# Griffin and attention trunk on one core: another loading order at the start, matmuls of ones ahead, and the first row sum two units later

## The chip, the cores and the metric

The kernel runs on one core of one Trainium2 chip. The metric is the device time of one execution in microseconds. All inputs and weights are fp32 and lie in HBM; about 404 MB are read in each execution.

## What is computed

A trunk of two layers works on T = 288 tokens (32 of a running stream, 256 of a new prompt) with a width of 2048. Layer 0 mixes with a gated linear recurrence, layer 1 with differential attention; a gated MLP with a short convolution follows each. Only layer 0's mixer is touched by the change:

```python
def rms_norm(x, g):
    return x * rsqrt(mean(x * x, -1) + EPS) * g

def rglru_mixer(x, conv_hist, h0, w_in, conv_w, conv_b, gate_w, gate_b, log_lam, w_out):
    u = x @ w_in                                   # x after rms_norm; 2048 -> 4096
    y = gelu(u[..., :2048])                        # "g" tiles
    full = concat([conv_hist, u[..., 2048:]])      # "r" tiles
    xc = causal_dwconv(full, conv_w, conv_b)       # width 4
    g = sigmoid(einsum('btnc,ncd->btnd', blocks(xc), gate_w) + gate_b)
    r, i = halves of g
    log_a = -8 * r * softplus(-log_lam)
    a = exp(log_a); b = sqrt(-expm1(2 * log_a)) * i * xc
    h_t = a_t * h_(t-1) + b_t                      # linear recurrence over the tokens
    return (h * y) @ w_out
```

## The kernel before

The width of 2048 is kept as 16 chunks of 128 partitions, so x is 16 tiles of 128x288; a DMA brings two chunks, 288 KB, and x0 to x7 below are these pairs. To reach fp32 accuracy, every operand is cut into a high and a low part, and each chunk of a product takes three matmuls into one PSUM bank: high by high (L967), weight-high by x-low (L968), weight-low by x-high (L969).

The weights stream once. They come in **units** of 2, 4 or 8 chunks of one output tile. For each unit SP issues the load (L840, tiles `w` for the small units 0 to 7, a ring of four `wr` buffers from unit 8 on), ACT rounds the high part (`cut_hi`, L845, `wh`), DVE subtracts it for the low part (`cut_lo`, L850, `wl`), and PE runs the unit's matmuls: 24 for a unit of 8 chunks. The chunks of x are cut in the same way at the start: `xh` on ACT (L144, scaled by the norm constants in `crg`) and `xl` on DVE (L147). The norm's own factor is applied later, when a tile leaves PSUM.

The main loop runs over the units in order. At unit i it issues the load of unit i+5, ACT's cut of unit i+3, then all side work that is due at i (`S.run_due(i)`, from a table filled with `S.at` and `S.chain`), then DVE's cut of unit i+3, then the matmuls of unit i. Each engine works off its own list in that order, so side work that stands ahead of a cut delays it, and with it the unit three further on.

The first four output tiles (r0, r1, g0, g1) are interleaved: units 0 to 3 are their first 2 chunks, 4 to 7 the next 2, 8 to 11 the next 4 and 12 to 15 the last 8. Their four PSUM banks come free only after the norm's factor is known: squares of x (`first_sq`, L157 on ACT, added up on DVE at L161), a matmul with ones over all partitions (`norm_row`, L205 and L206), and an inverse root on DVE (L181 to L198). `norm_row` is due at unit 14. From unit 16 on a tile is two units of 8 chunks (r2, r3, r4, r5, g2, g3, r6, r7, and so on).

Behind each r tile n stands a chain of stages: s1 evacuates PSUM (L330, L331) and loads the gate weights, s2 is the convolution (three DVE operations at L340 behind one on ACT), s3 and s4 cut its result and the gate weights (`xch`, `gwh` on ACT, `gwl`, `xcl` on DVE), s6 runs six gate matmuls (L362 to L364), s7 is four ACT operations with the sigmoid table, s8 a reciprocal on DVE (L379), s9 one ACT operation, s10 (odd n) a square root with its own table (L393), s11 the scans on DVE (L400, L402). Behind a g tile stands the gelu (L422), with a third table. `ACT_TABLE_LOAD` is the change from one of these tables to another.

Before the loop, ACT's queue issues the loads of x0, of the first norm constants `crg`, of x1, and later x2 and x3; SP's queue issues units 0 to 7, the rest of `crg`, units 8 to 11 and then x4 to x7. `coef` (due at unit 5) works out constants of the recurrence on ACT, POOL and DVE. In `psS` lie two PSUM banks for scores, which in layer 0 serve the gates of even tiles as `gate_ps`.

Of the kernel before, what the change touches and what calls it, by code (L numbers as in the profile page):

```python
# [11 lines left out]
F32 = mybir.dt.float32  # L12
# [6 lines left out]
P = 128  # L19
D = 2048  # L20
NS, NP = 32, 256
T = NS + NP
KC = D // P
# [6 lines left out]
LAM0 = 0.8 - 0.6 * math.exp(-0.3 * 1)  # L30
SCALE = 128.0 ** -0.5

REC_W = 296
REC_N = 292
REC_P = 36
# [61 lines left out]
def trunk(ctx, tc, d, prefetch=5, ahead=3):  # L97
    nc = tc.nc
    S = Stream()
# [7 lines left out]
    psA = ctx.enter_context(tc.tile_pool(name="psA", bufs=2, space=bass.MemoryType.PSUM))  # L107

    xx = [main.tile([P, 2 * T], F32, tag=f"x{c}", name=f"x{c}") for c in range(KC // 2)]
    x = [xx[c // 2][:, (c % 2) * T:(c % 2 + 1) * T] for c in range(KC)]  # L110
    xh = [main.tile([P, T], F32R, tag=f"xh{c}", name=f"xh{c}") for c in range(KC)]
# [42 lines left out]
    def first_sq(c):  # L154

        t = rgp.tile([P, 2 * T], F32, tag="ssw", name="ssw", bufs=1) if c == 0 else (nvz, srb)[c % 2]
        nc.scalar.activation(t, xx[c], AF.Square)  # L157
        if c == 0:
            acc_box["w"], acc_box["a"], acc_box["b"] = t, t[:, 0:T], t[:, T:2 * T]
        else:  # L160
            nc.vector.tensor_add(acc_box["w"], acc_box["w"], t)  # L161
# [41 lines left out]
    def norm_row(key):  # L203
        ps = psA.tile([P, 512], F32, tag="A", name="ssq_ps")
        nc.tensor.matmul(ps[:, :T], ones, acc_box["a"], start=True, stop=False)  # L205
        nc.tensor.matmul(ps[:, :T], ones, acc_box["b"], start=False, stop=True)  # L206
        rb_box["r"], *steps = rsqrt_steps(ps[:, :T], D, "rb")
        for f in steps:
            f()
        S.done.add((key, "r"))  # L210
# [108 lines left out]
    def rec_done(n):  # L319
        def done(i, ps):  # L320
# [62 lines left out]
                e["a"] = rgp.tile([P, REC_N], F32, tag="a", name="a", bufs=4)  # L383
                nc.scalar.activation(e["a"], e["q"], AF.Copy, scale=2.0, bias=-1.0)

            w = (1, 2, 1, 1)[n] if n < 4 else 0
            stages = [(1, s1), (2, s2), (3, s3), (4, s4)]
            stages += [(t + w, f) for t, f in ((6, s6), (7, s7), (8, s8), (9, s9))]
            if k == 1:
                def s10():  # L390
# [15 lines left out]
                        S.done.add(("hs", q))  # L406
                    return f
                stages += [(10 + w, s10), (11 + w, s11(n - 1)), (12 + w, s11(n))]
            S.chain(i + (1 if n < 2 else 0), *stages)
        return done  # L410

    def gate_done(n):
        def done(i, ps):
            e = {}
            k = n % 2

            def s1():
                e["y"] = rgp.tile([P, T], F32, tag="y", name="y", bufs=4)
                evac_scaled(e["y"], ps[:, :T], "n0")

            def s2():
                nc.scalar.activation(e["y"], e["y"], AF.Gelu_apprx_tanh)  # L422

            def s3():
                nc.gpsimd.tensor_mul(e["y"], e["y"], rgs[n]["hs"])

            def s4():
                nc.scalar.activation(Hh[n], e["y"], AF.Copy)

            def s5():  # L430
                nc.vector.tensor_sub(Hl[n], e["y"], r32(Hh[n]))  # L431
                S.done.add(("H0", n))
            w = 0 if k else 2
            S.at(i + 1, s1)
            S.at(i + 2 + w, s2)
            due = [i + 3 + w]

            def poll():
                if ("hs", n) in S.done:
                    s3()  # L440
                    S.chain(due[0], (1, s4), (2, s5))
                else:
                    due[0] += 1
                    S.at(due[0], poll)
            S.at(due[0], poll)
        return done
# [291 lines left out]
    def need_of(key):  # L738
        return lambda k: (key, k)

    order = [("r", 0), ("r", 1), ("g", 0), ("g", 1), ("r", 2), ("r", 3)]
    for n in range(4, KC, 2):
        order += [("r", n), ("r", n + 1), ("g", n - 2), ("g", n - 1)]
    order += [("g", KC - 2), ("g", KC - 1)]
    tiles = [tile_units(d["w_in"], n + (KC if w == "r" else 0), 0, [8, 8] if n >= 2 else [2, 2, 4, 8],
                        xh, xl, need_of("n0"), rec_done(n) if w == "r" else gate_done(n))
             for w, n in order]
    phase(tiles, 4)

    def open_pool(name, old):  # L750
# [101 lines left out]
    def cutw(u):  # L852
        cut_hi(u)
        cut_lo(u)

    nc.vector.memset(ones, 1.0)
    for b in recbuf:
        nc.gpsimd.memset(b, 0.0)

    def load_x(eng, *pairs):  # L860
        for c in pairs:
            eng.dma_start(xx[c], d["x"][c])

    def split_x(a, b):
        for c in range(a, b):
            norm_hi(c, rg("norm", c))
            norm_lo(c, rg("norm", c), "n0")

    def square_x(a, b):
        for c in range(a // 2, b // 2):  # L870
            first_sq(c)

    def coef():

# [14 lines left out]
        nc.gpsimd.tensor_scalar(o, l, -4.0, 0.0, op0=OP.mult, op1=OP.max)  # L889
        nc.gpsimd.tensor_add(o, o, q)  # L890

    load_x(nc.scalar, 0)
    nc.scalar.dma_start(crg[:, 0:KC], d["p_rg"][:, 0:KC])
    load_x(nc.scalar, 1)
    for i in range(12):
        tag = "hs" if i < 4 else "y"
        load(units[i], rgp.tile([P, T], F32, tag=tag, name="w0", bufs=4) if i < 8 else None)
        if i == 7:
            nc.sync.dma_start(crg[:, KC:], d["p_rg"][:, KC:])
    load_x(nc.sync, 4, 5, 6, 7)  # L900
    make_identity(nc, ident)
    cutw(units[0])
    split_x(0, 2)
    load_x(nc.scalar, 2)
    cutw(units[1])
    load_x(nc.scalar, 3)
    for u in units[2:4]:
        cutw(u)

    def side_loads():  # L910
# [9 lines left out]
        nc.vector.tensor_scalar(lam[:, 3:4], lam[:, 2:3], -LAM0, None, op0=OP.add)  # L920
        nc.vector.tensor_scalar(subc, rg("sub", 0, 2), 1.0 - LAM0, None, op0=OP.mult)

    for t, c, n in ((1, 2, 2), (3, 4, 2), (5, 6, 2), (7, 8, 4), (8, 12, 4)):
        S.at(t, lambda c=c, n=n: split_x(c, c + n))
    for t, c, n in ((9, 0, 4), (10, 4, 4), (11, 8, 4), (12, 12, 4)):
        S.at(t, lambda c=c, n=n: square_x(c, c + n))
    S.at(5, coef)
    S.at(14, lambda: norm_row("n0"))
    S.at(24, side_loads)
    S.at(40, lam_setup)  # L930

# [147 lines left out]
```

## Time and profile before

| | us |
|---|---|
| median of three runs (2507.55 to 2507.96) | 2507.75 |
| the profiled execution | 2507.55 |
| its span (first to last instruction) | 2505.7 |
| PE busy | 2480.6 (99%) |
| DVE busy | 1626.6 (65%) |
| ACT busy | 1198.3 (48%) |
| share of PE in the chain that ended last | 96% |

The profiled execution is 1.85 us longer than its span; that part lies outside all instructions. "Busy" counts an engine's instructions on their own, so PE at 99% says that hardly any time is left between matmuls, wherever they wait. Which stretch holds what is left is told by the list of PE's waits and by the timeline, where the bracket behind an instruction is the idle time ahead of it and what released it.

### The profile page before, as it was taken

What the parts mean: (1) busy time and instruction counts of PE and PEld (TensorE: products, weight loads), DVE (VectorE), ACT (ScalarE), POOL (GpSimd) and SP (SyncE); (2) the same over time, 40 slices, a digit from 0 to 9 for tenths busy, and PEclk for the clock granted to TensorE, in tenths of its full rate; (3) what the DMA queues carried; (4) which work ended last, traced back from release to release, by engine and by line L of the source; (5) the groups of instructions that cost most, each with busy time, mean ns of one, the idle gap of its engine ahead of it and who ended that gap; (6) DMA issues with size and microseconds to landing.
All of it is one profiled execution on the core that took longest, in us unless ns stands there. A gap on an engine that the chain in (4) does not pass through costs nothing.

```text
span 2505.7 us, 45997 instructions
## 1 busy us (share of the span) xinstructions
PE 2480.6 (99%) x18567; PEld 2474.0 (99%) x18567; DVE 1626.6 (65%) x2596; ACT 1198.3 (48%) x1749; POOL 279.0 (11%) x770
## 2 busy tenths in 40 slices
PE   8999999999999999999999999999999999999997
PEld 8999999999999999999999999999999999999997
DVE  8987666666446666555677677766666446666543
ACT  6887444444334444444445444544444334444442
POOL 3544110000000000011000000210000000000021
PEclk9999999999999999999999999999999999999999
DMA  6444444444554444555544553544445554444553
GB/s 227 165 163 163 168 163 164 165 166 159 166 166 169 165 164 168 158 164 174 181 161 161 176 171 115 194 161 168 163 165 161 164 170 165 166 165 164 162 168 115
DMA packets 126358, 414.36 MB, mean 165 GB/s; under 512 B 14400, under 2 KB 22976, under 8 KB 126144
## 3 DMA queue, kind: packets, MB, share of 16 engines
q1 hardware_dynamic: 124416, 409.39, 49.6%
q8 instruction: 145, 2.38, 0.4%
q10 hardware_dynamic: 1728, 2.02, 0.2%
q14 instruction: 69, 0.57, 0.1%
HBM read 403.86 MB, written 7.50 MB: 164 GB/s over the span
## 4 chain that ended last, share of the span: by engine, by line
PE 96%; DVE 1%; ACT 1%; issue 0%; DMA 0%; POOL 0%; ACTq 0%; DVEq 0%; POOLq 0%
PE acc L967 31%; PE acc L969 31%; PE acc L968 31%; DVE wl L850 0%; ACT wh L845 0%; PE os_ps L689 0%; PE spare L967 0%; DMA crg<-p_rg 0%; PE spare L969 0%; PE spare L968 0%; PE osq_ps L718 0%; PE sc_ps L557 0%; PE sc_ps L555 0%; PE sc_ps L556 0%; PE gate_ps L363 0%
## 5 line engine op out<-in xcount | busy, mean ns | idle before, releaser
L845 ACT ACTIVATE wh<-wr 128x1024 fp32r<-128x1024 f32 (+2 forms) x776 | 799.3, 1030 | 1206.4 <-PE acc L968 850.9
L850 DVE TENSOR_TENSOR wl<-wr,wh 128x1024 fp32r<-128x1024 f32 (+2 forms) x776 | 925.3, 1193 | 510.1 <-ACT wh L845 509.5
L967 PE MATMUL acc<-xh,wh 128*128 128x288 f32 x4096 | 1217.3, 297 | 6.2 <-ACT xh L144 6.2
L968 PE MATMUL acc<-xl,wh 128*128 128x288 f32 x4096 | 1209.6, 295 | 0.0
L969 PE MATMUL acc<-xh,wl 128*128 128x288 f32 x4096 | 1206.0, 294 | 2.5 <-DVE wl L850 2.5
L969 PEld LDWEIGHTS acc<-xh,wl 128*128 128x128 f32 x4096 | 772.3, 189 | 3.5 <-DVE wl L850 3.4
L967 PEld LDWEIGHTS acc<-xh,wh 128*128 128x128 f32 x4096 | 768.8, 188 | 6.8 <-ACT xh L144 6.2
L968 PEld LDWEIGHTS acc<-xl,wh 128*128 128x128 f32 x4096 | 770.0, 188 | 0.8 <-DVE xl L147 0.3
L968 PE MATMUL acc<-Hl,wh 128*128 128x288 f32 x1504 | 443.9, 295 | 0.8 <-DVE Hl L431 0.8
L967 PE MATMUL acc<-Hh,wh 128*128 128x288 f32 x1504 | 444.4, 295 | 0.0
L969 PE MATMUL acc<-Hh,wl 128*128 128x288 f32 x1504 | 442.9, 294 | 0.0
L968 PEld LDWEIGHTS acc<-Hl,wh 128*128 128x128 f32 x1504 | 282.3, 188 | 1.3 <-DVE Hl L431 1.2
L969 PEld LDWEIGHTS acc<-Hh,wl 128*128 128x128 f32 x1504 | 283.0, 188 | 0.0
L967 PEld LDWEIGHTS acc<-Hh,wh 128*128 128x128 f32 x1504 | 281.8, 187 | 0.1
L473 DVE SCALAR_TENSOR_TENSOR c<-up,cff,c 128x290 f32<-128x290 f32 x352 | 182.7, 519 | 6.2
L467 POOL COPY st_ff<-up 128x2 f32<-128x2 f32 x176 | 34.7, 197 | 1339.1 <-DVE up L463 1339.1
L462 DVE TENSOR_TENSOR up<-acc,srb 128x32 f32<-128x32 f32 x176 | 33.7, 192 | 128.7 <-PE acc L969 128.7
L967 PE MATMUL acc<-Hhx,wh 128*128 128x288 f32 x384 | 113.7, 296 | 0.0
L968 PE MATMUL acc<-Hlx,wh 128*128 128x288 f32 x384 | 113.3, 295 | 0.0
L969 PE MATMUL acc<-Hhx,wl 128*128 128x288 f32 x384 | 112.9, 294 | 0.0
L465 ACT ACTIVATE c<-up,cff 128x290 f32<-128x290 f32 x176 | 108.6, 617 | 0.7 <-DVE up L463 0.7
L172 POOL TENSOR_TENSOR srb<-srb,sq 128x288 f32<-128x288 f32 x56 | 62.0, 1107 | 287.0 <-ACT sq L165 281.4
(227 smaller groups left out, 1651.5 us busy)
## 6 DMA issues: line engine op xcount, KB each, us to landing
wr<-w_up SPq DMA_DIRECT2D x352, 512.0 KB, 3.7
wr<-w_dn SPq DMA_DIRECT2D x128, 448.0 KB, 3.3
wr<-w_qkv SPq DMA_DIRECT2D x96, 512.0 KB, 4.3
wr<-w_dn SPq DMA_DIRECT2D x64, 512.0 KB, 3.5
wr<-w_in SPq DMA_DIRECT2D x60, 512.0 KB, 3.8
wr<-w_rg_out SPq DMA_DIRECT2D x32, 512.0 KB, 3.7
wr<-w_at_out SPq DMA_DIRECT2D x24, 512.0 KB, 4.3
wr<-w_at_out SPq DMA_DIRECT2D x16, 256.0 KB, 3.2
```

The lines of the kernel that those rows point to most:

```text
L172: nc.gpsimd.tensor_add(acc_box["a"], acc_box["a"], sq)
L462: nc.vector.tensor_mul(buf[:, 2:34], ps[:, 0:NS], rb[:, 0:NS])
L465: nc.scalar.activation(c, buf[:, 0:UP_N], AF.Identity, scale=ff(f"w{l}", f), bias=ff(f"b{l}", f))
L467: nc.gpsimd.tensor_copy(st_ff[:, f, 0, :], buf[:, 290:292])
L473: nc.vector.scalar_tensor_tensor(c, buf[:, t:t + UP_N], ff(f"w{l}", t * 2 * NF + f), c, op0=OP.mult, op1=OP.add)
L845: nc.scalar.activation(u["wh"][:, :n], u["raw"][:, :n], AF.Copy)
L850: nc.vector.tensor_sub(u["wl"][:, :n], u["raw"][:, :n], r32(u["wh"])[:, :n])
L967: nc.tensor.matmul(o, wh, h, start=u["first"] and z == 0, stop=False)
L968: nc.tensor.matmul(o, wh, lo, start=False, stop=False)
L969: nc.tensor.matmul(o, wl, h, start=False, stop=u["last"] and z == nk - 1)
```

## The change

- ACT's queue issues the norm constants first, then the two halves of x0. All the other x pairs move to SP's queue, between the weights: x1 after unit 3, x2 and x3 after unit 7 (then the rest of `crg`), x4 after unit 9, x5 after unit 10, x6 and x7 after unit 11.
- Seven fp32 matmuls of ones with ones, 128 columns each, are PE's first work. Their bank is not read.
- The cuts of x8 to x15 (chunks) go to units 7, 8, 9 and 10, two each; they stood at 7 and 8, four each. The squares are due one by one at units 11, 11, 12, 12, 13, 14, 14 and 15; they stood in pairs at 9 to 12.
- `norm_row` is due at unit 16 (`ROW0`), not 14. The fifth and sixth output tiles (r2 and r3, units 16 to 19) accumulate in the two `psS` banks.
- The stages of r0 to r5 get new due times, and `gate_done` counts from unit 15 at the earliest. The gate matmuls of r0 to r7, which were due at units 20, 22, 24, 26, 27, 29, 35 and 37, are due at 22, 24, 26, 28, 30, 32, 35 and 37; the reciprocals follow two units behind.

The core of the diff:

```diff
+ROW0 = 16
...
-            w = (1, 2, 1, 1)[n] if n < 4 else 0
-            stages = [(1, s1), (2, s2), (3, s3), (4, s4)]
+            w = (1, 2, 3, 3, 1, 1)[n] if n < 6 else 0
+            v = w if n > 1 else 0
+            stages = [(1, s1), (2, s2), (3 + v, s3), (4 + v, s4)]
...
-            S.chain(i + (1 if n < 2 else 0), *stages)
+            S.chain((ROW0 - 1, ROW0, i, i, i + 2, i + 2)[n] if n < 6 else i, *stages)
...
             w = 0 if k else 2
+            i = max(i, ROW0 - 1)
             S.at(i + 1, s1)
...
-                        xh, xl, need_of("n0"), rec_done(n) if w == "r" else gate_done(n))
-             for w, n in order]
+                        xh, xl, need_of("n0"), rec_done(n) if w == "r" else gate_done(n),
+                        t - 4 if t in (4, 5) else None)
+             for t, (w, n) in enumerate(order)]
...
+    warm = psA.tile([P, 512], F32, tag="A", name="warm")
+    for _ in range(7):
+        nc.tensor.matmul(warm[:, 0:P], ones, ones, start=True, stop=True)
...
-    load_x(nc.scalar, 0)
     nc.scalar.dma_start(crg[:, 0:KC], d["p_rg"][:, 0:KC])
-    load_x(nc.scalar, 1)
+    for c in range(2):
+        nc.scalar.dma_start(x[c], d["x"][0][:, c * T:(c + 1) * T])
...
-        if i == 7:
+        if i == 3:
+            load_x(nc.sync, 1)
+        elif i == 7:
+            load_x(nc.sync, 2, 3)
             nc.sync.dma_start(crg[:, KC:], d["p_rg"][:, KC:])
-    load_x(nc.sync, 4, 5, 6, 7)
+        elif i in (9, 10):
+            load_x(nc.sync, i - 5)
+    load_x(nc.sync, 6, 7)
...
-    for t, c, n in ((1, 2, 2), (3, 4, 2), (5, 6, 2), (7, 8, 4), (8, 12, 4)):
+    for t, c, n in ((1, 2, 2), (3, 4, 2), (5, 6, 2), (7, 8, 2), (8, 10, 2), (9, 12, 2), (10, 14, 2)):
         S.at(t, lambda c=c, n=n: split_x(c, c + n))
-    for t, c, n in ((9, 0, 4), (10, 4, 4), (11, 8, 4), (12, 12, 4)):
-        S.at(t, lambda c=c, n=n: square_x(c, c + n))
+    for c in range(KC // 2):
+        S.at((11, 11, 12, 12, 13, 14, 14, 15)[c], lambda c=c: first_sq(c))
     S.at(5, coef)
-    S.at(14, lambda: norm_row("n0"))
+    S.at(ROW0, lambda: norm_row("n0"))
```

**SP's queue at the program's start.** `w` and `wr` are weights of units, `x_` a pair of x (the number names an instance, x_78 being x0), `crg` constants. Before:

```order
L840 DMA w_174<-w_in 128x256
L840 DMA w_176<-w_in 128x256
L840 DMA w_178<-w_in 128x256
L840 DMA w_180<-w_in 128x256
L840 DMA w_182<-w_in 128x256
L840 DMA w_184<-w_in 128x256
L840 DMA w_186<-w_in 128x256
L840 DMA w_188<-w_in 128x256
L899 DMA crg<-p_rg 128x226
L840 DMA wr<-w_in 128x512 x4
L862 DMA x_82<-x 128x576
L862 DMA x_83<-x 128x576
```

After:

```order
L845 DMA w_182<-w_in 128x256
L845 DMA w_184<-w_in 128x256
L845 DMA w_186<-w_in 128x256
L845 DMA w_188<-w_in 128x256
L871 DMA x_79<-x 128x576
L845 DMA w_191<-w_in 128x256
L845 DMA w_193<-w_in 128x256
L845 DMA w_195<-w_in 128x256
L845 DMA w_197<-w_in 128x256
L871 DMA x_80<-x 128x576
L871 DMA x_81<-x 128x576
L907 DMA crg<-p_rg 128x226
```

The x loads now stand among the weights that are used at the same time, x2 and x3 ahead of unit 8's weights.

**DVE around the row sum.** `ssw` adds up the squares, L181 to L198 (L182 to L199 after) are the inverse root, `rec` is the first evacuation. Before:

```order
L161 TENSOR_TENSOR ssw<-ssw,srb 128x576
L850 TENSOR_TENSOR wl<-wr,wh 128x1024 x2
L181 TENSOR_SCALAR nvz<-ssq_ps 128x288
L184 TENSOR_SCALAR srb<-nvz 128x288
L189 TENSOR_TENSOR nvz<-srb 128x288
L190 TENSOR_TENSOR nvz<-nvz 128x288
L191 SCALAR_TENSOR_TENSOR nvz<-nvz 128x288
L192 SCALAR_TENSOR_TENSOR srb<-nvz,srb 128x288
L196 TENSOR_TENSOR nvz<-srb 128x288
L197 SCALAR_TENSOR_TENSOR nvz<-nvz 128x288
L198 SCALAR_TENSOR_TENSOR srb<-nvz,srb 128x288
L330 TENSOR_TENSOR rec_165<-acc,srb 128x32
```

After:

```order
L162 TENSOR_TENSOR ssw<-ssw,srb 128x576
L855 TENSOR_TENSOR wl<-wr,wh 128x1024
L182 TENSOR_SCALAR nvz<-ssq_ps 128x288
L185 TENSOR_SCALAR srb<-nvz 128x288
L190 TENSOR_TENSOR nvz<-srb 128x288
L191 TENSOR_TENSOR nvz<-nvz 128x288
L192 SCALAR_TENSOR_TENSOR nvz<-nvz 128x288
L193 SCALAR_TENSOR_TENSOR srb<-nvz,srb 128x288
L197 TENSOR_TENSOR nvz<-srb 128x288
L198 SCALAR_TENSOR_TENSOR nvz<-nvz 128x288
L199 SCALAR_TENSOR_TENSOR srb<-nvz,srb 128x288
L331 TENSOR_TENSOR rec_165<-acc,srb 128x32
```

The last addition stood two weight cuts ahead of the inverse root; now it stands one cut ahead, and all of it two units later in the program.

**ACT about units 28 and 29.** `t` is the square root, `y` the gelu, `xch` and `gwh` are s3 and `r`, `ip`, `t`, `q`, `a` the set with the sigmoid table. Before:

```order
L393 ACT_TABLE_LOAD
L393 ACTIVATE t<-t 128x292 x2
L345 ACTIVATE xch<-xc 128x292
L140 ACTIVATE gwh<-gwr 128x256
L845 ACTIVATE wh<-wr 128x1024
L370 ACT_TABLE_LOAD
L370 ACTIVATE r<-gate_ps,crg 128x292
L371 ACTIVATE ip<-gate_ps,crg 128x292
L373 ACTIVATE t<-r,spc 128x292
L375 ACTIVATE q<-t 128x292
L384 ACTIVATE a<-q 128x292
```

After:

```order
L396 ACT_TABLE_LOAD
L396 ACTIVATE t<-t 128x292 x2
L850 ACTIVATE wh<-wr 128x1024
L425 ACT_TABLE_LOAD
L425 ACTIVATE y<-y 128x288
L346 ACTIVATE xch<-xc 128x292
L141 ACTIVATE gwh<-gwr 128x256
L425 ACTIVATE y<-y 128x288
L371 ACT_TABLE_LOAD
L371 ACTIVATE r<-gate_ps,crg 128x292
L372 ACTIVATE ip<-gate_ps,crg 128x292
L374 ACTIVATE t<-r,spc 128x292
```

A gelu with its table load now stands between the square root and the cuts `xch` and `gwh`, and a second one behind them.

## Rows read from the trace of the kernel before

**Rows 1.** Timeline of PE, start: begin, duration, instruction, [idle before <-releaser].

```profile
6.24 0.61 PE L967 MATMUL acc<-xh,wh 128*128 128x288 f32 x1 [6.24 <-ACT xh L144]
...
12.23 0.30 PE L969 MATMUL acc<-xh,wl 128*128 128x288 f32 x1
12.36 0.29 PE L967 MATMUL acc<-xh,wh 128*128 128x288 f32 x1
...
16.35 0.40 PE L969 MATMUL acc<-xh,wl 128*128 128x288 f32 x1 [0.38 <-DVE wl L850]
```

**Rows 2.** Timeline of PE, units 12 and 14.

```profile
24.50 0.40 PE L969 MATMUL acc<-xh,wl 128*128 128x288 f32 x1 [1.03 <-DVE wl L850]
...
31.42 0.75 PE L205 MATMUL ssq_ps<-ssw,ones 128*128 128x288 f32 x2 [0.52 <-DVE ssw L161]
32.01 0.65 PE L206 MATMUL ssq_ps<-ssw,ones 128*128 128x288 f32 x2
32.28 0.51 PE L967 MATMUL acc<-xh,wh 128*128 128x288 f32 x1
```

**Rows 3.** Timeline of PE, units 34 and 37.

```profile
102.57 0.40 PE L969 MATMUL acc<-xh,wl 128*128 128x288 f32 x1 [0.85 <-DVE wl L850]
...
114.39 0.40 PE L363 MATMUL gate_ps<-xcl,gwh 128*128 128x292 f32 x1 [1.14 <-DVE xcl L350]
```

**Rows 4.** Timeline of ACT, start.

```profile
5.65 0.96 ACT L144 ACTIVATE xh<-x,crg 128x288 fp32r<-128x288 f32 x2 [0.52 <-DMA crg<-p_rg]
...
13.27 0.63 ACT L845 ACTIVATE wh<-wr 128x512 fp32r<-128x512 f32 x1 [0.42 <-DVE wl L850]
```

**Rows 5.** Two windows: each engine's busy us (instructions), PEclk, DMA share, GB/s.

```profile
0.00:12.00 12.00, 5.76 (x23) 5.50 (x23) 4.43 (x12) 6.34 (x14) 1.27 (x8) 1.00 0.77 239
12.00:16.00 4.00, 3.97 (x29) 3.73 (x28) 2.99 (x8) 3.43 (x9) 0.44 (x2) 1.00 1.00 362
```

**Rows 6.** Timeline of DVE around units 8 and 12.

```profile
15.66 1.25 DVE L850 TENSOR_TENSOR wl<-wr,wh 128x512 fp32r<-128x512 f32 x2
...
22.53 0.76 DVE L161 TENSOR_TENSOR ssw<-ssw,srb 128x576 f32<-128x576 f32 x1 [0.97 <-ACT srb L157]
23.21 1.24 DVE L850 TENSOR_TENSOR wl<-wr,wh 128x1024 fp32r<-128x1024 f32 x1
```

**Rows 7.** DMA issues, 16.3 to 16.5 us: count, size, median us to landing.

```profile
wr<-w_in SPq DMA_DIRECT2D x1, 512.0 KB, 3.8
```

**Rows 8.** Timeline of DVE, first evacuation of a recurrent tile.

```profile
37.94 0.41 DVE L331 TENSOR_TENSOR rec<-acc,srb 128x256 f32<-128x256 f32 x1
```

**Rows 9.** Timeline of DVE, units 26 to 35.

```profile
64.76 1.64 DVE L340 SCALAR_TENSOR_TENSOR xc<-rec,crg,xc 128x292 f32<-128x292 f32 x3 [0.37 <-ACT xc L333]
...
67.45 1.97 DVE L379 RECIPROCAL q<-q 128x292 f32<-128x292 f32 x1
...
78.92 0.94 DVE L141 TENSOR_TENSOR gwl<-gwr,gwh 128x256 fp32r<-128x256 f32 x1 [2.00 <-ACT gwh L140]
79.78 0.45 DVE L239 TENSOR_TENSOR y<-acc,srb 128x288 f32<-128x288 f32 x1
80.15 1.21 DVE L850 TENSOR_TENSOR wl<-wr,wh 128x1024 fp32r<-128x1024 f32 x1
...
82.06 0.43 DVE L350 TENSOR_TENSOR xcl<-xc,xch 128x292 fp32r<-128x292 f32 x1
...
97.07 0.82 DVE L400 TENSOR_TENSOR_SCAN hs<-a,crg,ip 128x32 f32<-128x32 f32 x1 [0.78 <-POOL ip L394]
...
98.64 2.74 DVE L340 SCALAR_TENSOR_TENSOR xc<-rec,crg,xc 128x292 f32<-128x292 f32 x3 [0.15 <-ACT xc L333]
```

**Rows 10.** Timeline of ACT, units 28 to 31.

```profile
76.16 1.28 ACT L393 ACT_TABLE_LOAD   x1
...
88.53 0.78 ACT L422 ACTIVATE y<-y 128x288 f32<-128x288 f32 x2
...
89.89 1.04 ACT L845 ACTIVATE wh<-wr 128x1024 fp32r<-128x1024 f32 x1
```

More of the change, by code (lines that the diff above doesn't have):

```diff
@@ L867, in split_x @@
             norm_lo(c, rg("norm", c), "n0")
-    def square_x(a, b):
-        for c in range(a // 2, b // 2):
-            first_sq(c)
     def coef():
@@ L903, in trunk @@
     split_x(0, 2)
[L904 to L907, printed above, removed]
+    for u in units[1:4]:
         cutw(u)
```

## The prediction

> **What bounds the kernel now.** Read first the page's busy shares and the chain that ended last: PE is busy 99% of the span and the chain runs over PE for 96%. So only two things can move the time: idle time between matmuls, and matmuls that run slowly. The list of PE's waits sorts the idle time by what it waited for, the timeline says where each wait stands. What the change touches lies in the first 115 us, in two places.
>
> *The front*, up to unit 16. PE's first matmul starts at 6.24, behind the high cut of x. The 24th starts at 12.23 and the next at 12.36 [rows 1]: 23 spacings take 5.99 us, 0.26 each, against 0.13 between those two. This is the lower of the clock's two levels (1.2 GHz against 2.4) after an idle start; at 0.133 they would take 3.06, so it costs 2.93 us. PE then waits 0.38 for unit 8 at 16.35, 1.03 for unit 12 at 24.50, and 0.52 for the last addition of squares at 31.42 [rows 1, 2].
>
> *The middle*, units 26 to 37. PE waits 0.85 for unit 34 at 102.57 and 1.14 for a gate at 114.39 [rows 3]. After that no wait belongs to the parts that change.
>
> In both places PE is fed by a queue that cannot be made shorter by making PE faster: what is gained ahead of a wait is given back at the wait. So the forecast follows the last wait of each place, not the sum of all of them.
>
> **Part by part.**
>
> *Constants first, x0 in halves.* ACT's first cut of x begins at 5.65 after 0.52 us of waiting for `crg`, which was issued second [rows 4]. Issued first it lands earlier by one issue, at most those 0.52, while the half of x0 is issued where `crg` stood. PE's first matmul moves to about 5.75 to 5.9. By the rule above this is given back unless unit 8 comes earlier too.
>
> *Seven matmuls of ones.* No such matmul stands in the trace. Bounds: the pair of fp32 matmuls of 288 columns at L205 takes 0.59 from start to start of the next pair (31.42 to 32.01), so 0.3 each [rows 2]; at the lower clock twice that, 0.6. Seven at no more than 0.6 are 4.2 us, and since they need only a tile of ones they end before 5.75: they lie wholly in time in which PE stands still, cost 0. What they can bring is the clock: between 0 and 2.93 us on PE itself. The granted clock column is no help, it reads 1.00 for the first 12 us, where the spacing says half [rows 5]; hence I read the level from the spacing alone. That the engine was idle ahead of its slow stretch and had worked through it when it sped up is what [rows 1] show.
>
> The Trainium skill, "TensorE: Matmul & The Clock Gate", section "What's actually happening", says that the default state is throttled and activity releases it; by that rule PE reaches its first real matmul at full speed. The trace agrees on the order of things (slow first, fast after work). By that rule alone, without the next limit, the sum would be 2.9 us better.
>
> *The next limit: unit 8.* Its weights are cut on ACT at 13.27, its matmul starts at 16.35 [rows 1, 4]: 3.1 us, in which ACT cuts x6 and x7 and the constants of `coef`, and DVE gets to `wl` at 15.66 only behind a reciprocal that waits for POOL [rows 6]. None of this is moved: the order of ACT and DVE in this stretch is the same. What can come earlier is the cut at 13.27, and that follows the landing. 2.6 MB must land before it (units 0 to 8, x0 to x3, the constants); before, 239 GB/s over the first 12 us make 2.87 MB, and from 12 to 16 the DMA engines are 1.00 busy at 362 GB/s [rows 5]. The same bytes come in an order that only puts x ahead: 2.6 MB have landed at 10.9 by the mean rate, and I allow a spread to 12.2. The matmul of unit 8 can then stand at 14.9 to 15.4 with a fast clock. If the clock stays low until 12, the buffers of the small units hold ACT back (the cut at 13.27 itself waited 0.42 for DVE), and it comes at 15.6 to 15.7. So the warm-up, worth 2.93 on PE, is worth some 0.5 at unit 8.
>
> *Unit 12, the last wait of the front.* Its load needs the buffer that unit 8's low cut frees, at 16.3, and took 3.8 us to land [rows 7], at 20.2; the matmul that waits for its low cut starts at 24.50 [rows 2], 4.3 later. The change frees the buffer 0.65 (low clock) to 1.4 us (high) earlier. Behind the landing, one addition of squares no longer stands ahead of this cut on DVE; it held the queue from 22.53 to 23.21 [rows 6], and its square on ACT goes too: 0.6. Together 1.25 to 2.0. Against it, DMA is saturated until about 18 us by the same bytes, with x6 and x7 ahead of this load now as before; that takes up to 0.3. I take 1.4, range 0 (the landing does not move) to 2.0. Everything won earlier is inside this number.
>
> *Row sum at unit 16.* PE had nothing to do from 30.90 (31.42 less 0.52), and the next unit's matmul starts at 32.28, 1.38 later; since matmuls overlap by 0.16 (0.29 long, 0.13 apart), the loss is 1.54 [rows 1, 2]. The four row sum matmuls themselves take 0.86 of it (31.42 to 32.28) and are still to be done, the remaining 0.68 is the wait. Two units later the last addition is due at unit 15, one cut ahead of the row sum, and done some 2.4 us into that unit's 3.2 of matmuls: gain 0.68, bounds 0 and 0.68.
>
> *Two tiles in the score banks.* The inverse root begins behind the row sum, and the first tile was evacuated by 38.35, 6 us after the row sum [rows 2, 8]. With the row sum at unit 16 the four old banks come free about two units into the next tile; r2 and r3 have banks of their own until unit 20, 12.8 us after. Cost 0; without that cover PE would stand still for about 5 us. The banks are wanted again by the first gate at unit 22, when the evacuation of r3 at 20 is done with a margin of about 1.5 us: 0 again, with the price of a rival below.
>
> *New due times in the middle.* The work of DVE and ACT is the same, its order is not. Before, at unit 28, a table load of 1.28 and two roots stood ahead of `xch` and `gwh`, and DVE waited 2.00 for `gwh` [rows 9, 10]. Now a weight cut (1.04), another table load (1.28) and one gelu (0.39, half of the two in 0.78) stand between, 2.7 more; DVE has an evacuation (0.37, 79.78 to 80.15) and a cut (1.1) of its own in that time [rows 9], so its wait grows to 2.00 + 2.7 − 1.5, some 3.1. In return the reciprocals (1.97 at 67.45) come every second unit and not in consecutive ones, and two pairs of scans (with the cut ahead of them 1.9, 80.15 to 82.06, so 0.8 alone) move behind unit 36. I walked DVE's list from the start of unit 29 to the gate of the last of the eight tiles, and take each item from rows 9. Unit 29: the wait of 3.1, `gwl`, scans and cut: 5.7. Unit 30: `xcl` 0.4, reciprocal 1.9, scans and cut 1.9, evacuation 0.4, a wait for POOL like the 0.78 at 97.07: 5.4. Unit 31: a low cut 0.4, three convolution operations 1.6, cut 1.1: 3.1. Unit 32: reciprocal 1.9, two small cuts 0.8, evacuation 0.4, cut 1.1, and a wait of about half the earlier one for `gwh`, again behind a table load and roots: 5.8. Unit 33: scans 0.8, `xcl` 0.4, convolution 1.6, cut 1.1: 3.9. Unit 34: reciprocal 1.9, scans 0.8, two small ones 0.8, cut 1.1: 4.6. With the last `xcl` that is +28.9. PE gets there after eight units of 3.2 (24 matmuls 0.133 apart), three gates of 0.8 and one matmul: +28.1. So 0.8 us of stall stays by undisturbed durations, and about 2.0 by the disturbed ones (the three convolution operations took 2.74 at 98.64 against 1.64 at 64.76). Before, the two waits were 1.99, and restarting the row of matmuls behind each adds 0.1 to 0.3 (the first one lasts 0.40, not 0.29) [rows 1, 3]: 2.3 to 2.6. I take 1.3 left of 2.5: gain 1.2, bounds 0 and 2.6.
>
> The Trainium skill, "SBUF — State Buffer", section "Who interferes with whom", says that DVE operations with two SBUF inputs contend with GpSimd reading SBUF; the 2.74 against 1.64 fits it, no run here isolates it. By that rule the stalls would stay near 2.0, since POOL keeps all its multiplications in this stretch.
>
> **Sum.** 1.4 + 0.68 + 1.2 = 3.3 us. The profiled execution took 2507.55, its span 2505.7 with 1.85 around it, and is 0.2 below the median of 2507.75. 2507.55 − 3.3 gives **2504.3 us**. What a measurement of this kernel can tell from no change is about 0.2%, 5 us: the forecast is inside that.
>
> **The rivals.**
>
> *Everything works.* The clock is high from the first matmul, the loads come by the upper rate, and the longer spacing of reciprocals removes both waits of the middle. For it: the waits of rows 3 stand where DVE's reciprocals came in consecutive units, and the new due times part them. Front 1.7, row sum 0.68, middle 2.6: 5.0, 2502.6. Against it: ACT's stretch at unit 29. Chance 0.20.
>
> *The clock is not raised* (the ones end too early, or don't count): the change doesn't do this part of what it says. Unit 8 at 15.6 to 15.7 and a front of 1.2: 2504.5. It lies within the forecast and has no chance of its own. By the rule of the clock page the front would be 1.7, 2504.0.
>
> *The middle gains nothing.* The wait for `gwh` at unit 29 eats what the spread of reciprocals gives. Front and row sum alone are 2.1, or 1.6 with a low clock: 2505.7. For it: DVE's added 1.1 of waiting is longer than half of what the middle has to give. Chance 0.24.
>
> *Slower.* The pile on ACT at unit 29 (cut, two table loads, two gelus, `xch`, `gwh` and a set of sigmoids) lasts about 7 us; the units' own cuts stand behind it, ACT gets one such unit behind, and DVE waits for ACT's high cut as well as for `gwh`. It decides from the point at which stalls of units 29 to 37 exceed 2.5 + 2.1 = 4.6 us; a whole further unit of lag (3.2) on top of the 2.0 gives 5.2, a loss of 0.6: 2508.2. To pass 0.2% it would have to be three such units. Chance 0.06.
>
> **How the numbers follow.** Forecast 0.50, everything works 0.20, middle without gain 0.24, slower 0.06. The forecast's own case reaches from 2503.2 to 2505.2. Its neighbours are 2502.6 and 2505.7; with the bounds of the front (0 to 2.0) around them, 2502.0 to 2506.8 holds 8 in 10. Faster by over 0.2% means under 2502.7: most of the first rival, 0.17, and 0.03 from the forecast's low end, 0.20. Slower by over 0.2%, over 2512.8: 0.03. Within: 0.77.
>
> **What would show it.** Right: the first real matmul at 5.7 to 5.9 and spacings of 0.13 from there; then a wait of PE for unit 8 of more than 2 us at about 15; the wait of unit 12 at 22.8 to 23.3; no wait at L206 for `ssw`; unit 16 at 36 to 37.5; a wait of DVE for `gwh` at unit 29 of 2 to 3 us; PE waits of 0.8 to 2 between units 34 and 37. Wrong: unit 8 at 13 (then DMA was not the limit, and the front gives up to 4), a wait of the gate at unit 22 for a bank, or PE waits of over 3 us after unit 29.

## The result: slower by half a per cent

The changed kernel takes 2520.34 us (median of four runs, 2518.63 to 2520.96) against 2507.65 (2507.51 to 2507.96) before: a ratio of 1.0051, 95% interval 1.0039 to 1.0063. The forecast was 2504.3 with a range of 2502.0 to 2506.8; it was wrong in sign. The profiled execution took 2520.96, its span 2519.2, 13.5 more than before.

PE's waits over the span of the changed kernel (what waited, for what, us in total, times, longest):

```profile
PE spare L974 <- DVE rec L332: 5.9, 1, 5.9
PE gate_ps L364 <- DVE xcl L351: 5.1, 3, 3.2
PE acc L976 <- DVE wl L855: 4.2, 3, 2.0
...
PE gate_ps L363 <- ACT gwh L141: 0.3, 1, 0.3
```

The first line is new, 5.9 us in one piece. The second was 1.1 before ([rows 3] has it at 114.39), on the other gate matmul. The timeline of PE says where they are (begin, duration, instruction, idle before):

```profile
5.28 0.40 PE L974 MATMUL acc<-xh,wh 128*128 128x288 f32 x1 [0.87 <-ACT xh L145]
...
12.30 0.40 PE L976 MATMUL acc<-xh,wl 128*128 128x288 f32 x1 [0.72 <-DVE wl L855]
...
15.64 0.40 PE L976 MATMUL acc<-xh,wl 128*128 128x288 f32 x1 [1.48 <-DVE wl L855]
...
24.38 0.40 PE L976 MATMUL acc<-xh,wl 128*128 128x288 f32 x1 [2.02 <-DVE wl L855]
...
39.28 0.51 PE L974 MATMUL spare<-xh,wh 128*128 128x288 f32 x1
...
51.95 0.58 PE L974 MATMUL spare<-xh,wh 128*128 128x288 f32 x1 [5.90 <-DVE rec L332]
52.33 0.44 PE L975 MATMUL spare<-xl,wh 128*128 128x288 f32 x1
...
113.48 0.41 PE L363 MATMUL gate_ps<-xch,gwh 128*128 128x292 f32 x1 [0.33 <-ACT gwh L141]
...
117.14 0.47 PE L364 MATMUL gate_ps<-xcl,gwh 128*128 128x292 f32 x1 [3.25 <-DVE xcl L351]
...
147.72 0.40 PE L364 MATMUL gate_ps<-xcl,gwh 128*128 128x292 f32 x1 [1.59 <-DVE xcl L351]
```

Unit 16 starts at 39.28, against 38.87 before: the front has won nothing in this execution. Then r3's first matmul, unit 18, stands still for 5.90 at 51.95. The gate at unit 35 waits 0.33 and 3.25, one further on 1.59. Behind three of these places matmuls start 0.24 apart, not 0.13, for 14 or 15 matmuls. Here the granted clock shows it (three stretches of the changed kernel: length, busy us of PE, PEld, DVE, ACT and POOL with counts, then granted clock, DMA share, GB/s):

```profile
25.30:28.50 3.20, 3.20 (x16) 3.20 (x15) 2.77 (x3) 3.20 (x6) 0.00 (x0) 0.50 0.72 250
52.00:55.90 3.90, 3.90 (x16) 3.90 (x17) 0.93 (x1) 0.53 (x1) 1.22 (x3) 0.50 0.76 242
117.20:120.70 3.50, 3.50 (x15) 3.50 (x16) 3.43 (x5) 3.46 (x7) 1.78 (x2) 0.52 0.45 150
```

0.50 is the lower of the clock's two levels, 1.2 GHz. In the first 12 us of the kernel before the column read 1.00 at the same spacing ([rows 1, 5]); for that stretch the spacing alone tells it.

**The sum of the 13.5 us**, from starts of matmuls less the usual 0.13: front 0.4; unit 18, 6.1 for the wait and 0.3 for the next start, 1.65 for 15 spacings at the low clock: 8.0; middle 0.5 + 3.5 + 1.75 + 0.45 for four gate waits (the last is 0.28 at 155.47) and 1.6 for 15 slow spacings: 7.8; less 2.55 for the two waits before that are gone [rows 3]. 0.4 + 8.0 + 7.8 − 2.55 = 13.65, which is 0.15 over the 13.5 measured.

### The profile page after: what moved, and what is told of

Its sections match the earlier page's. It is cut to its first block, busy times and chain, and to the rows that moved or that the text cites. A ratio compares the mean times of both kernels' runs of the same rounds, so it can differ in the third digit from the quotient of the medians.

```text
span 2519.2 us, 46029 instructions
## 1 busy us (share of the span) xinstructions
PE 2486.8 (99%) x18581; PEld 2479.3 (98%) x18581; DVE 1628.4 (65%) x2596; ACT 1198.1 (48%) x1749; POOL 271.4 (11%) x770
## 4 chain that ended last, share of the span: by engine, by line
PE 94%; DVE 3%; ACT 1%; DMA 1%; issue 1%; POOL 0%; SPq 0%; DVEq 0%; ACTq 0%; POOLq 0%
PE acc L974 31%; PE acc L976 30%; PE acc L975 30%; DVE wl L855 1%; DVE q L380 0%; DMA wr<-w_in 0%; PE spare L974 0%; DVE xc L341 0%; PE spare L976 0%; PE spare L975 0%; ACT wh L850 0%; PE os_ps L693 0%; DVE gwl L142 0%; DVE hs L405 0%; DMA x<-x 0%
```

## Why r3 waits for r2: two banks in one tile

DVE between the row sum and that wait, changed kernel:

```profile
39.70 0.46 DVE L182 TENSOR_SCALAR nvz<-ssq_ps 128x288 f32<-128x288 f32 x1 [0.74 <-PE ssq_ps L207]
...
44.10 0.41 DVE L332 TENSOR_TENSOR rec<-acc,srb 128x256 f32<-128x256 f32 x1
...
46.39 0.41 DVE L332 TENSOR_TENSOR rec<-acc,srb 128x256 f32<-128x256 f32 x1
...
49.40 1.63 DVE L341 SCALAR_TENSOR_TENSOR xc<-rec,crg,xc 128x292 f32<-128x292 f32 x3
...
51.38 0.41 DVE L332 TENSOR_TENSOR rec<-spare,srb 128x256 f32<-128x256 f32 x1
```

The inverse root starts at 39.70, the evacuation of r0 is done at 44.5 and that of r2 only at 51.8, behind the evacuations of g0, g1 and r1, the convolutions of r0 and r1, two cuts of weights and one of gate weights. PE starts r3 0.16 after it. r3 writes the second bank and r2 the first, so there is no data between them. But both are halves of one two-bank tile, and the program's own list has the wait: of the first matmuls of the four units in these banks only r3's (the third line) waits for a semaphore (a counter that one engine raises and another waits for) of DVE, and the count that it wants is the one that r2's evacuation brings it to.

```
L974 MATMUL spare_614<-xh0_86,wh_487 128x288 [waits Activation_49]
L974 MATMUL spare_614<-xh8_94,wh_519 128x288 [waits Activation_49]
L974 MATMUL spare_614<-xh0_86,wh_553 128x288 [waits DVE_49,Activation_49]
L974 MATMUL spare_614<-xh8_94,wh_585 128x288 [waits Activation_49]
```

The trace of before had this wait, elsewhere and small: the attention's output projection uses the same two halves, and its list of PE's waits has the line

```profile
PE spare L967 <- DVE x L273: 0.6, 1, 0.6
```

(L273 evacuates the tile in the first half). There DVE did the evacuation at once, and the price was 0.6 us.

**e1: two tiles.** r2 and r3 accumulate in the two buffers of the pool `psA`, each a tile of its own; the rest is the changed kernel.

```diff
-                        t - 4 if t in (4, 5) else None)
+                        -1 if t in (4, 5) else None)
...
+            elif bank < 0:
+                u["st"]["ps"] = psA.tile([P, 512], F32, tag="A", name="spare")
```

> The changed kernel, but r2 and r3 (units 16 to 19) accumulate in two tiles of the two-buffer pool psA instead of the two halves of one psS tile. Theory A (the 5.9 us wait at unit 18 is a dependency on the shared tile: r3's first matmul waits until DVE has evacuated r2): the wait and the 16 matmuls at the lower clock behind it go, 5.9 + 0.3 + 1.8 = 8 us, so about 2512.5 us, and no PE wait near unit 18. Rival B (DVE is the limit after the row sum, whatever the banks): PE runs ahead at unit 18 and gives it back at the gates of units 22 to 35, total within 2 us of 2520.3.

Measured: 2512.0 us (ten runs, 2510.89 to 2513.56), 8.3 less than the changed kernel. Theory A holds. DVE evacuates r2 just as late, 12.1 us behind the start of unit 16 (51.38 less 39.28 in the changed kernel, 48.88 less 36.78 here), and the list of PE's waits has no line for `rec` any more (DVE's evacuation of r2, then a line of PE's waits, e1):

```profile
48.88 0.41 DVE L332 TENSOR_TENSOR rec<-spare,srb 128x256 f32<-128x256 f32 x1
```

```profile
PE gate_ps L364 <- DVE xcl L351: 5.1, 3, 3.2
```

The gates' waits are as long as in the changed kernel. Rival B expected DVE's lateness to come back there; it does not. The two profiles are 10.0 us apart, as unit 16 starts 2.5 earlier in e1's; the price of the tile is the 8.0 of the sum and the 8.3 of the medians.

**e4: the late part alone** (the kernel before with its loads, cuts of x and no matmuls of ones, but the new squares, row sum, banks and due times).

> The kernel before with its own loads and cuts of x and no matmuls of ones, but with the new squares, row sum at unit 16, shared score banks and due times. Theory A (nearly all of the loss is made behind the row sum): the wait of r3 for r2's evacuation of about 6 us and the gate waits are there, 2507.6 + 11.5 = 2519. Rival B (the clock that fell in the front carries over and the late part alone is harmless): under 2512.

Measured: 2520.2 us (four runs, 2519.39 to 2521.19), all of the loss; theory A named its places and said 2519. r3 waits 5.89, the gate at unit 35 3.25, with slow matmuls behind each.

## Why the gates are late: due times and a copy on POOL

The gate at unit 35 waits for `gwh` and `xcl` of r6. Upstream of it, ACT and POOL of the changed kernel:

```profile
105.80 0.63 ACT L334 ACTIVATE xc<-rec,crg 128x292 f32<-128x292 f32 x1 [4.18 <-POOL rec L328]
...
110.71 1.28 ACT L396 ACT_TABLE_LOAD   x1
...
113.03 0.40 ACT L141 ACTIVATE gwh<-gwr 128x256 fp32r<-128x256 f32 x1
```

```profile
102.37 1.15 POOL L381 TENSOR_TENSOR ip<-ip,q 128x292 f32<-128x292 f32 x1 [1.23 <-DVE q L380]
103.47 1.18 POOL L408 COPY st_h<-hs 128x2 f32<-128x2 f32 x1
104.61 1.03 POOL L428 TENSOR_TENSOR y<-y,hs 128x288 f32<-128x288 f32 x1
105.59 0.18 POOL L328 COPY rec<-crg 128x3 f32<-128x3 f32 x1
```

At unit 30 ACT needs r6's evacuated tile with three halo columns, copied on POOL (L328). That copy stands behind a reciprocal's product (L381), a copy of states and a gelu product (L428), until 105.59, and ACT waits 4.18 us. The table load, the roots, `xch` and `gwh` of unit 32 follow, so `gwh` ends at 113.4, when PE is there already.

**e7: the halo copy on ACT**, on top of e1.

```diff
-                nc.gpsimd.tensor_copy(buf[:, 0:3], rg("hist", 3 * n, 3))
+                nc.scalar.activation(buf[:, 0:3], rg("hist", 3 * n, 3), AF.Copy)
```

> The kernel with two psA tiles for r2 and r3, and in stage s1 the copy of the three halo columns into rec (L328) on ACT, not on POOL. Theory A (the gate at unit 35 is late because ACT waited 4.2 us at unit 30 for that copy, which stood on POOL behind the multiplies of scans, and the table load, the roots and gwh of unit 32 stand behind it): ACT's wait goes, the 0.3 + 3.25 us of PE's waits at unit 35 fall under 0.5 and no slow matmuls follow them, 5 us less than 2512.0: 2507. Rival B (ACT's table loads and DVE's list are late without POOL too): the wait at unit 35 stays over 2 us and the time over 2510.

Measured: 2510.41 us (2509.29 to 2511.87), 1.6 less than e1, not 5. ACT's wait for POOL is gone, the gate at unit 35 waits 2.00, and now that at unit 37 waits 1.36 (PE, e7):

```profile
107.10 0.40 PE L364 MATMUL gate_ps<-xcl,gwh 128*128 128x292 f32 x1 [2.00 <-DVE xcl L351]
...
115.92 0.40 PE L364 MATMUL gate_ps<-xcl,gwh 128*128 128x292 f32 x1 [1.36 <-DVE xcl L351]
```

So the copy was a part, about 1.6 us with its `gwh` wait, and rival B is right on the rest: DVE's own list is late. The two waits further on stay too (1.79 at 138.22 and 0.28 at 145.97); nothing here traces them to their cause.

**e10: the row sum back at unit 14.** On top of e7, squares at units 9 to 12 and the row sum at 14, as before the change; the new due times stay.

```diff
-        S.at((11, 11, 12, 12, 13, 14, 14, 15)[c], lambda c=c: first_sq(c))
+        S.at((9, 9, 10, 10, 11, 11, 12, 12)[c], lambda c=c: first_sq(c))
...
-    S.at(ROW0, lambda: norm_row("n0"))
+    S.at(14, lambda: norm_row("n0"))
```

> The kernel of e7 (two psA tiles for r2 and r3, halo copy on ACT) with the squares at units 9 to 12 and the row sum at unit 14, as before the change, but with the new due times of the stages. Theory A (the new due times themselves pack scans, reciprocals and cuts so that the gates at units 35 and 37 come late): PE's waits there stay near 2.0 and 1.4 us, the time within 1 us of 2510.4. Rival B (DVE is late there because its inverse root and evacuations start two units later): the waits fall under 1.0 in all, 2507.5 or less.

Measured: 2513.27 us. The two waits (PE, e10) are those of e7 to 0.02:

```profile
107.86 0.40 PE L364 MATMUL gate_ps<-xcl,gwh 128*128 128x292 f32 x1 [2.02 <-DVE xcl L351]
...
116.68 0.40 PE L364 MATMUL gate_ps<-xcl,gwh 128*128 128x292 f32 x1 [1.34 <-DVE xcl L351]
```

So they are made by the new due times, not by the two units by which the inverse root is later. Theory A has the waits right and the time wrong: the 2.9 us over e7 come from elsewhere, and not all of it was traced. The two profiles are 1.3 apart (e7's is its slowest execution, 1.5 over its median): unit 16 starts at 39.93 against 38.98, after a wait of 2.40 for unit 12, for which the next section has the reason, and another stretch at the low clock, 1.5 us, follows the wait of 1.78 at 138.98, where e7 has none.

What the due times do can be read on DVE in the changed kernel:

```profile
86.16 1.81 DVE L855 TENSOR_TENSOR wl<-wr,wh 128x1024 fp32r<-128x1024 f32 x1
87.90 1.03 DVE L142 TENSOR_TENSOR gwl<-gwr,gwh 128x256 fp32r<-128x256 f32 x1
...
99.26 1.08 DVE L351 TENSOR_TENSOR xcl<-xc,xch 128x292 fp32r<-128x292 f32 x1
...
106.47 1.64 DVE L341 SCALAR_TENSOR_TENSOR xc<-rec,crg,xc 128x292 f32<-128x292 f32 x3 [1.50 <-ACT xc L334]
...
113.46 0.92 DVE L142 TENSOR_TENSOR gwl<-gwr,gwh 128x256 fp32r<-128x256 f32 x1 [2.02 <-ACT gwh L141]
...
116.65 0.43 DVE L351 TENSOR_TENSOR xcl<-xc,xch 128x292 fp32r<-128x292 f32 x1
```

A weight cut takes 1.81 and not 1.22, `gwl` 1.03 and not 0.42, `xcl` 1.08 and not 0.46: beside each of these POOL runs a product (L381 at 86.08, L377 at 87.61 and 98.33). It is not so beside every product: the weight cuts at 98.14 and 108.02 took 1.19 and 1.22 beside L377, and there L377 itself took 1.69 and 1.68, not 1.03. The Trainium skill, "SBUF — State Buffer", section "Who interferes with whom", says that a DVE operation with two SBUF inputs contends with a GpSimd operation that reads SBUF; these rows agree, though no run took the products away. Reciprocals at units 28, 30 and 32, and scans at 29 and 30 put these products beside the cuts for units 31 to 35. How much of the lateness these pairs make is argued from the rows, not shown by a run. No run has the gates' old due times with the row sum at unit 16; e9 below has them with the row sum at unit 15, and one wait of 1.05 there.

**e8: the halo copy on ACT in the kernel before**, and nothing else.

> The kernel before, only with the halo copy on ACT. Theory A: before, ACT waited 2.5 and 2.3 us for POOL in the same place; if that holds the middle up there too, the waits of 0.85 and 1.14 at units 34 and 37 shrink, 2506.5 to 2505.5. Rival B (in the old order the copy is off the path): 2507.6, waits as they were.

Measured: 2506.04 us (2505.50 to 2507.78) against 2507.59, ratio 0.9995, interval 0.9985 to 1.0005. The wait for unit 34 at 102.57 [rows 3] is gone, the one at unit 37 stays:

```profile
113.01 0.40 PE L363 MATMUL gate_ps<-xcl,gwh 128*128 128x292 f32 x1 [1.07 <-DVE xcl L350]
```

The runs are lower by 1.5 in the median, inside theory A's range; the interval does not exclude no change.

## The front: what is won is given back

**e2: the changed kernel without the matmuls of ones.**

> The changed kernel without the seven matmuls of ones. Theory A (unit 12's landing sets the front, and PE's longer waits ahead of it, 0.7 + 1.5 + 2.0 us, are what let the clock fall at 25.4 us): the first matmuls are slow, the waits shrink to under 1.5 in all, unit 12 stays at 24.4 +- 0.3, no slow matmuls behind it: 1.6 us less, 2518.7. Rival B (the warm-up is worth its 2.9 us): 2523.

Measured: 2520.15 us, within 0.2 of the changed kernel. The warm-up is worth nothing here, by neither theory's number: rival B's 2.9 us are not lost, and theory A's 1.6 us are not won in the median. The first matmuls are slow, and PE comes to unit 12 at the same 24.38 (PE, e2):

```profile
15.46 0.40 PE L972 MATMUL acc<-xh,wl 128*128 128x288 f32 x1 [0.93 <-DVE wl L855]
...
24.38 0.40 PE L972 MATMUL acc<-xh,wl 128*128 128x288 f32 x1 [2.01 <-DVE wl L855]
```

The low clock behind unit 12, 1.6 us, is absent in this profile, though the wait ahead of it is as long, 2.01; in the changed kernel 0.72 and 1.48 went before it, here only 0.93.

**e6: the matmuls of ones alone**, on the kernel before.

> The kernel before with the seven matmuls of ones alone. Theory A (PE is faster at first and gives it back at unit 8 and unit 12): spacings of 0.13 from the start, the waits ahead of unit 13 grow by about 2.5 us together, 2507.5 +- 0.5, or 2509 where the clock falls behind unit 12 as in the changed kernel. Rival B (the 2.9 us are kept): 2504.7.

Measured: 2507.78 us (2506.85 to 2508.44) against 2507.59: no change. Theory A on the time, but not on the spacings. The seven matmuls are 14 instructions in the trace, 3.36 us from 1.05 on, and PE then waits 1.36 for x. The first real matmuls are 0.13 apart, and from 7.76 to 11.12 they are 0.24 apart; here the granted clock shows it (two stretches of e6, columns as above):

```profile
5.70:7.50 1.80, 1.58 (x9) 1.31 (x10) 1.37 (x3) 1.18 (x5) 0.00 (x0) 1.00 0.97 258
7.60:11.10 3.50, 3.50 (x16) 3.50 (x16) 2.38 (x6) 2.18 (x6) 0.00 (x0) 0.52 0.93 300
```

e1, e7 and e10 have 10, 18 and 19 such spacings between 6.1 and 10.6, the changed kernel's own profile and e3 none. In e1, e7 and e10 the first real matmul lasts 0.61 already, as at 6.24 in [rows 1] without any ones, and 0.40 in the other three. So in three of six profiles the ones have not raised the clock when the real work starts, and in a fourth (e6) it falls again; no run shows what decides it. e1 had the slow start and won its front all the same, the changed kernel the fast one and did not.

**e5: the loading order alone.**

> The kernel before with the new loading order alone (norm constants first, x0 in halves, x1 to x7 on SP's queue); cuts of x, squares, row sum, banks and due times as before, no matmuls of ones. Theory A (unit 12's landing and its cuts decide the front, not the order of x): 2507.3 +- 0.6. Rival B (the x loads ahead of unit 8's weights hold them up): PE's wait for unit 8 over 1 us and 2508.5.

Measured: 2508.08 us (2506.59 to 2509.17): by the median 0.5 over before and 0.2 above theory A's range; the spread of the runs does not separate it from no change. Unit 8 waits 1.23 in its profile, at 15.51 though, 0.84 earlier than before, so not rival B.

**e3: loads, ones and spread cuts of x together.**

> The kernel before with the new loading order, the seven matmuls and the spread cuts of x, but with its own squares, row sum at unit 14, banks and due times. Theory A (the front gains nothing at unit 12 and loses the clock for 3 us behind it): 2507.6 + 1.5 = 2509. Rival B (the prediction's front, 1.4 better): 2506.2.

Measured: 2508.67 us (2507.85 to 2509.59), 1.1 over before; ratio 1.0005, interval 0.9996 to 1.0014. Theory A by the number: unit 12 waits 2.47 (PE, e3), and 14 slow spacings follow.

```profile
24.68 0.40 PE L975 MATMUL acc<-xh,wl 128*128 128x288 f32 x1 [2.47 <-DVE wl L850]
```

**What sets unit 12** is two things: when its weights land, and what ACT and DVE do between the landing and its low cut.

*The landing.* Issued at 15.6 to 15.7, the load took (512 KB, us to landing) in the changed kernel and in e1:

```profile
wr<-w_in SPq DMA_DIRECT2D x1, 512.0 KB, 4.9
```

```profile
wr<-w_in SPq DMA_DIRECT2D x1, 512.0 KB, 4.0
```

In e1 the matmul of unit 12 that waits comes at 23.39 (22.8 to 23.3 was predicted), and unit 16 at 36.78, 2.1 earlier than before: 1.1 at unit 12 and 1.0 behind it, where the sum had 1.4 and 0.68. Over the thirteen profiles (the kernel before, the changed one, e1 to e11) the load took from 3.7 (e6) to 6.0 (e5) and landed between 19.5 and 21.5, and the landing does not follow the issue: issued first, at 15.24 (e4), it landed at 20.50, issued last, at 16.37 (before), at 20.19. None shows why.

*Behind the landing.* ACT and then DVE, changed kernel:

```profile
20.72 1.06 ACT L850 ACTIVATE wh<-wr 128x1024 fp32r<-128x1024 f32 x1 [3.05 <-DMA wr<-w_in]
21.68 0.94 ACT L145 ACTIVATE xh<-x,crg 128x288 fp32r<-128x288 f32 x2
...
22.24 0.95 DVE L148 SCALAR_TENSOR_TENSOR xl<-x,crg,xh 128x288 fp32r<-128x288 f32 x2 [3.09 <-ACT xh L145]
23.11 1.22 DVE L855 TENSOR_TENSOR wl<-wr,wh 128x1024 fp32r<-128x1024 f32 x1
```

From the start of ACT's high cut of unit 12 to PE's matmul at 24.38 it is 3.66 us, because the low cut of two chunks of x, which the change moved to unit 9, stands on DVE ahead of that of the weights and waits for ACT's high cut of the same chunks. In e4, with the new squares but the cuts of x where they were, it is 2.37 (ACT and PE, e4):

```profile
20.61 1.06 ACT L850 ACTIVATE wh<-wr 128x1024 fp32r<-128x1024 f32 x1 [1.27 <-DVE wl L855]
...
22.98 0.40 PE L970 MATMUL acc<-xh,wl 128*128 128x288 f32 x1 [0.47 <-DVE wl L855]
```

All thirteen profiles sort by these two parts of the change (us from the start of that high cut to that matmul):

| | cuts of x as before | cuts of x spread to units 7 to 10 |
|---|---|---|
| squares at units 9 to 12 | 4.18 to 4.21 (before, e5, e6, e8, e9) | 5.05 and 5.07 (e3, e10) |
| squares from unit 10 or 11 on | 2.37 (e4, e11) | 3.66 to 3.68 (changed kernel, e1, e2, e7) |

So the later squares win 1.4 to 1.8 us at unit 12, and the spread cuts of x take 0.9 to 1.3 of it away. With the squares where they were, e3 is late at unit 12 although its load took only 3.9, so it does not measure the changed kernel's front. And e4, without the new loads, ones and cuts of x, starts unit 16 at 36.52, 2.35 earlier than before.

## A version that beats both

**e9** is the kernel before with the halo copy on ACT, r2 and r3 in two tiles of `psA`, and the row sum at unit 15; the gates keep their due times.

```diff
-            w = (1, 2, 1, 1)[n] if n < 4 else 0
+            w = (0, 1, 1, 1)[n] if n < 4 else 0
...
-            S.chain(i + (1 if n < 2 else 0), *stages)
+            S.chain(i + (2 if n < 2 else 0), *stages)
...
-    S.at(14, lambda: norm_row("n0"))
+    S.at(15, lambda: norm_row("n0"))
```

> The kernel before with the halo copy on ACT, two psA tiles for r2 and r3, and the row sum at unit 15, one unit later; loads, squares, due times of the gates as before. Theory A (the row sum's wait of 0.52 and its refill can be had without new due times): PE waits at L205 gone, middle waits as in e8, 2506.0 - 0.7 = 2505.3. Rival B (DVE's later start comes back at units 34 to 37): 2506.5 to 2508.

Measured: 2505.31 us (eleven runs, 2504.70 to 2506.12) against 2507.49, ratio 0.9991, interval 0.9982 to 0.9999, just clear of no change. Theory A: no wait for `ssw`, and one wait of 1.05 in the middle.

**e11** spreads the squares too, due at units 10, 10, 11, 11, 12, 13, 13 and 14.

> e9 with the squares due one by one at units 10, 10, 11, 11, 12, 13, 13 and 14, not in pairs at 9 to 12. Theory A (additions of squares stand ahead of unit 12's low cut, 0.7 us): unit 12 starts 0.6 earlier, 0.5 us less than e9. Rival B (unit 12 is set by its landing, or the later additions hold the row sum again): within 0.3 of e9 or slower.

Measured: 2504.99 us (2504.64 to 2505.41), ratio 0.9990, interval 0.9981 to 0.9999; 0.3 under e9, between theory A's 0.5 and rival B's bound. Unit 12 starts 1.2 earlier and waits 0.29, and the row sum waits 1.33, so the wait has moved to the last addition (PE, e11):

```profile
23.34 0.40 PE L972 MATMUL acc<-xh,wl 128*128 128x288 f32 x1 [0.29 <-DVE wl L851]
...
34.27 0.75 PE L205 MATMUL ssq_ps<-ssw,ones 128*128 128x288 f32 x2 [1.33 <-DVE ssw L161]
...
112.47 0.40 PE L363 MATMUL gate_ps<-xcl,gwh 128*128 128x292 f32 x1 [0.84 <-DVE xcl L350]
```

It is 2.5 us faster than before and 15.4 faster than the changed kernel.

## The prediction, step by step

The forecast was a gain of 1.4 for the front, 0.68 for the row sum and 1.2 for the due times, with the shared banks at 0. In the profile the front and the row sum together lost 0.4, the shared tile 8.0 and the due times 5.25. One of its signs of being wrong came, a wait of PE of over 3 us after unit 29 (3.25).

- *Two tiles in the score banks, cost 0*: this step failed, 8.0 of the 13.5 us, as e1 shows. It treated the two banks as free of each other, and weighed only when they are wanted by the gates; no rival carried it. The price it named, "about 5 us" without the cover, belongs to another wait (PE without a free bank), and that 5.9 came is near it by chance. The row that could have told, PE's 0.6 us for L273 in the attention's output projection, was in the list of waits.
- *New due times, gain 1.2*: the second failure, 7.8 lost against 2.55, so −5.2 (its bounds were 0 and 2.6). The walk followed DVE to the gate of the last tile, at unit 37, and left out the one at unit 35. By its own numbers `xcl` of r6 is done at +21.2 there and PE at +20.9; measured from the start of unit 29 at 92.2 (the gate of unit 30 at 95.39 less 3.2) it was done at +24.9. Its steps were each too short: +7.1 for 5.7, +12.3 for 11.1, +17.0 for 14.2, +23.7 for 20.0. The long operations beside POOL's products, which it added once as 1.1, came six times between 86 and 101, about 0.6 each, and ACT's wait of 4.18 for the halo copy was not in it. e10 shows that the due times make these waits, e7 what the copy adds; the share of POOL's products is argued.
- *The wait for `gwh` at unit 29, 3.1*: it did not come. DVE reached it late, at 95.84, without waiting; a wait of 2.02 came at unit 32.
- *The rival "slower"* named the right place and direction for the middle, at 2508.2, by ACT's pile at unit 29, which did not do it. With the middle's loss and without the tile's (e1) the time is 2512.0.
- *Constants first*: right in direction, more than was said: first matmul at 5.28 (5.75 to 5.9). The seven profiles with the new loading order have it at 5.16 to 5.43, the six with the old one at 5.54 to 6.24.
- *Matmuls of ones*: right that they are hidden and that the faster clock is given back at units 8 and 12 (e2, e6), also that they may not raise the clock (three of six profiles). Not foreseen: the clock can fall again, at 7.7 in e6, at 25.2 behind unit 12 in the changed kernel, 1.6 us there.
- *Unit 8* was put at 14.9 to 15.4 with a fast clock, and came at 15.64 with one.
- *Unit 12, 1.4*: the third failure, 0.1 came (24.38 against 24.50). The load was issued 0.7 earlier, as was said, and landed 0.4 later, 4.9 and not 3.8 after its issue; no profile shows that an earlier issue lands earlier. Behind the landing the 0.6 that was said came, 3.66 for 4.21, but by luck: the squares gave 1.8, and the spread cuts of x, which the working puts at nothing, took 1.3. That DMA is saturated until about 18 us does not hold either: before, its share is 0.58 and 0.55 in the two us from 16 to 18.
- *Row sum, 0.68*: right, no wait for `ssw` in the changed kernel.
- *Slips in the sums*, none of which turns the forecast: 2.00 + 2.7 − 1.5 is 3.2, not 3.1; the items of unit 29 add up to some 5.9, not 5.7; the rival without gain in the middle is 1.2 + 0.68 = 1.9 with a low clock, not 1.6 (its 2505.7 fits 1.9); and the x2 of L205 in [rows 2] is one fp32 matmul in two instructions, as the seven of ones are 14, so its bound for the ones had another base.

## To carry to other kernels

Before two accumulations share one tile of two banks, look for the wait of the second one's first matmul on the first one's evacuation: the dependency follows the tile. When work is moved away from ahead of a cut, look also for what the same change puts there. When due times are moved, check every consumer along the way and not only the last one, and look on POOL's list for small copies that stand behind long products. A queue that follows a landing or a long list gives back what PE wins ahead of it.

## What was not expected of the hardware

In the changed kernel the granted clock fell to 0.50 at 25.2, 0.8 us after PE had resumed from a wait of 2.02; inside the wait of 5.90 (it reads 1.00 from 46 to 49 and 0.50 from 49.1 on); and 0.2 us after PE had resumed from the wait of 3.25. The slow stretches of 13 to 15 spacings cost 1.4 to 1.65 us each. Over the thirteen profiles, between 12 and 170 us, no fall came with a wait of PE of up to 1.62 us; of eight waits from 1.78 to 2.02 three had one (2.02 in the changed kernel, 1.87 in e7, 1.78 in e10) and five had none (2.02 in e10, 2.01 in e2, 2.00 and 1.79 in e7, 1.92 in e9); all ten of 2.40 and longer had one. So a wait of about 2 us can cost 1.5 us beyond itself, and need not. The granted clock column reads 1.00 for the slow start of the kernel before and 0.50 for the later slow stretches: for a start the spacing of matmuls is the safer row. And unit 12's load of 512 KB, issued between 15.2 and 16.4 us, took from 3.7 to 6.0 us in the profiles of these thirteen kernels.
